# Input projection by Strassen's seven half products in two passes of 1024 tokens

## The chip, the cores and the metric

The kernel runs on one core of one Trainium2 chip. A core has TensorE (PE; its weight loads are shown as PEld), VectorE (DVE), ScalarE (ACT), GpSimd (POOL) and SyncE (SP), which here issues the DMAs. The metric is device time in microseconds (us) of one launch; lower is better.

## The reference

One inference step of a decoder layer in float32, for 2048 prompt tokens and 8 sampled tokens, model width 1024. Cut to what matters:

```python
u = _rmsnorm(h, pre_g) @ w_in                 # 1024 -> 11264 columns
aq, ak, av, az, bq, bf, bi, bz, cq, cz, ga, gb, gc = jnp.split(u, IN_OFFSETS, axis=-1)
# A: 3 groups of 8 heads of 64, (window, dilation) = (128,1), (512,4), (2048,16); rotary q, k
aq, ak = _rope(aq, pos), _rope(ak, pos)
for g in range(3):                            # 128-query blocks against (previous block, own block)
    o_g, lse_g = attend(g, aq[:, :, g], ak[:, :, g], av[:, :, g])
alpha = softmax(stack(lses)); ya = sum(alpha * outs) * silu(az)
# B: HGRN2 gated recurrence, 4 heads, state 128x128
ob, S_fin = _hgrn2(bq, (1 - lb) * sigmoid(-bf), bi, log(lb + (1 - lb) * sigmoid(bf)), S0)
yb = headnorm(ob) * silu(bz)
# C: cross-attention of 4 heads of 128 into 256 memory tokens
yc = softmax(cq @ mk.T * 128 ** -0.5) @ mv * silu(cz)
merged = sigmoid(ga) * (ya @ w_pa) + sigmoid(gb) * (yb @ w_pb) + sigmoid(gc) * (yc @ w_pc)
out = h + _rmsnorm(merged @ w_out, post_g)
```

The outputs are `out` for both kinds of tokens, the rotated keys and the values of the last rows of each window, the HGRN states and the memory's keys and values. Nearly all of the arithmetic is in the product of the first line.

## The kernel before

Every large product is made in high precision from three rounded ones: both factors are cut into a high part (rounded to F32R, the format that PE takes at full rate) and a low part (the rest), and `mm3` issues high x high, high x low and low x high for each of the eight slices of 128 input rows (lines L163 to L165). ACT makes the high part (L200 for weights) and POOL the low part (L201); for tokens these are L247 and L248.

The work goes in stages.

1. *Values* (V): eight units of 256 columns of `w_v`, token-major, tile by tile of 128 tokens. In the first two units the tokens are normalised on the way (`Prep`: squares, DVE reduction L231, a matmul with ones L233, `rsqrt` L145 to L149, eight DVE products L245, split). Memory keys and values come beside the next four units. The values of sampled tokens are small matmuls (L281).
2. *Queries and keys* (QK): 12 units of 256 columns of `w_t`, feature-major. A unit has two blocks of 128 features, each for five chunks of tokens (512, 384, 384, 384 and 392, the last with the sampled tokens), by lines L402 to L404:

```python
for k in range(KT):
    hi, lo = (t[:, k % 2, jc] for t in pieces[k // 2])
    T.matmul(ps[:, :w], lhsT=hi, rhs=xh[c][:, k, :], start=(k == 0), stop=False)
    T.matmul(ps[:, :w], lhsT=hi, rhs=xl[c][:, k, :], start=False, stop=False)
    T.matmul(ps[:, :w], lhsT=lo, rhs=xh[c][:, k, :], start=False, stop=(k == KT - 1))
    if k < KT - 1:
        yield 3 * w * PE_COL, None
```

   The rotation takes from PSUM, on DVE, a product with the cosines (L450) and a shuffle (L451), and then on POOL a product with the sines (L452) and an addition (L455).
3. *Gates* (G): 24 more units of `w_t`. Beside them, in this order, go attention (96 steps of two heads and two blocks of 128 queries), HGRN (4 heads x 4 spans of 512 tokens, 16 items), cross-attention (32 half steps), and the sampled tokens. A planner interleaves them on PE: each of these generators yields what its matmuls cost and the least time until its next turn (`ATT_GAP` and the like), and a loop issues side work as soon as it is due and projection matmuls otherwise. PE's order is the written order; the other engines' orders are made by the scheduler.
4. Branch products with the merge gates, then the output projection (again `mm3`, with L1276 and L1277 for the parts of its inputs).

An attention step loads queries and keys in float32 from DRAM and cuts them on DVE (high part of the queries L540, of the keys L544, low parts L545 and L546). Keys are stacked as [high; low] on the two halves of the partitions, so one matmul of all 128 rows makes two of the products (L575 and L576, eight a step). Then come the mask and minimum on DVE (L580), the exponential on ACT (L582), transposes on PE (L595) with a copy on ACT (L597), and products with the values, 64 columns wide (L611), copied by DVE (L614). After each pair of heads a merge (`merge`, L695 and others) weighs the three groups, with statistics `stC` and outputs `uT` that come back from DRAM.

PSUM has eight banks: three for the projection (`gps`), the others for the side work.

## Time and profile before

| | |
|---|---|
| Median of 3 runs | 3179.59 us (3176.21 to 3181.13) |
| Span of the profiled execution, from its first instruction to its last | 3169.3 us |
| Mean PE clock granted | 0.98 of full |
| Busy share of the span | PE 95%, PEld 87%, DVE 48%, ACT 31%, POOL 32% |
| DMA | 400 MB, queues busy 43% of the time of 16 engines |

No other time of the profiled execution is given; its span lies 10.3 us below the median of the runs. The busy time of PE is an end that the profile models, so the distance between the starts of matmuls is the better measure of their rate. A group line reads: line, engine, operation, tile written and tiles read, shapes, count | busy time, mean ns of one | time the engine stood idle just before them, and what ended it. A timeline row gives start and duration in us. In a row of waits the numbers are the total in us, the times, and the longest.

### The profile page before, as it was taken

The numbers are of one execution on the slowest core, as the hardware profiler recorded it, in microseconds if no ns is written. First come the engines' busy times: TensorE is split into PE (matmuls) and PEld (weight loads), VectorE is DVE, ScalarE is ACT, GpSimd is POOL, SyncE is SP. The second block draws the span as 40 slices with busy tenths as digits, with TensorE's granted clock in tenths as the row PEclk, the third lists the DMA queues.
The fourth block names the chain that finished last, engine by engine and source line by source line (L and its number), as shares of the span: only waits on it lengthen the run. The fifth ranks groups of instructions, "written<-read, shape, count | busy, mean of one in ns | idle before, by whom it ended". The sixth has DMA issues, their size and how long they took to land. (4 is left out here: it accounts for less than half of the span.)

```text
span 3169.3 us, 56318 instructions
## 1 busy us (share of the span) xinstructions
PE 3023.6 (95%) x21644; PEld 2768.5 (87%) x21644; DVE 1530.8 (48%) x3827; ACT 993.0 (31%) x2468; POOL 1021.2 (32%) x836
## 2 busy tenths in 40 slices
PE   6999999999999999999989999999998988999998
PEld 6999999999999987878878888888886778899986
DVE  8700002222224776777772277777757356233232
ACT  4412110000003654434552244444443433201222
POOL 4312126556663211111222231112125125634411
PEclk9999999999999999999989999999999999999999
DMA  4332222112123567767675323233246467665442
GB/s 137 103 97 88 72 78 75 68 67 80 67 80 111 134 168 188 170 170 191 166 170 153 108 88 97 84 99 98 89 127 180 116 164 216 199 175 176 156 146 95
DMA packets 383134, 400.11 MB, mean 126 GB/s; under 512 B 89416, under 2 KB 306120, under 8 KB 379536
## 3 DMA queue, kind: packets, MB, share of 16 engines
q1 hardware_dynamic: 382864, 396.50, 43.3%
q8 instruction: 170, 2.79, 0.4%
q14 instruction: 100, 0.82, 0.1%
HBM read 257.71 MB, written 138.67 MB: 125 GB/s over the span
## 5 line engine op out<-in xcount | busy, mean ns | idle before, releaser
L402 PE MATMUL bank<-rnd 128*128 128x384 f32 (+2 forms) x2880 | 1033.8, 359 | 13.8 <-ACT side L479 7.6
L404 PE MATMUL bank<-rnd 128*128 128x384 f32 (+2 forms) x2880 | 1010.1, 351 | 6.4 <-POOL rnd L201 6.4
L403 PE MATMUL bank<-rnd 128*128 128x384 f32 (+2 forms) x2880 | 1010.2, 351 | 0.0
L402 PEld LDWEIGHTS bank<-rnd 128*128 128x128 f32 x2880 | 550.3, 191 | 43.3 <-ACT side L479 7.9
L404 PEld LDWEIGHTS bank<-rnd 128*128 128x128 f32 x2880 | 548.3, 190 | 32.2 <-POOL rnd L201 7.6
L403 PEld LDWEIGHTS bank<-rnd 128*128 128x128 f32 x2880 | 549.6, 191 | 23.3 <-issue 1.9
L163 PE MATMUL bank<-rnd 128*128 128x256 f32 (+4 forms) x1648 | 532.4, 323 | 8.4 <-DVE raw L1249 4.2
L165 PE MATMUL bank<-rnd 128*128 128x256 f32 (+4 forms) x1648 | 529.2, 321 | 3.5 <-POOL rnd L248 3.4
L164 PE MATMUL bank<-rnd 128*128 128x256 f32 (+4 forms) x1648 | 529.5, 321 | 1.9 <-POOL rnd L1228 1.2
L201 POOL TENSOR_TENSOR rnd<-raw,rnd 128x512 fp32r<-128x512 f32 x172 | 227.7, 1331 | 557.2 <-ACT rnd L200 550.9
L163 PEld LDWEIGHTS bank<-rnd 128*128 128x128 f32 (+1 forms) x1648 | 313.4, 190 | 25.2 <-ACT rnd L1214 3.6
L165 PEld LDWEIGHTS bank<-rnd 128*128 128x128 f32 (+1 forms) x1648 | 313.4, 190 | 17.3 <-POOL rnd L248 4.6
L164 PEld LDWEIGHTS bank<-rnd 128*128 128x128 f32 (+1 forms) x1648 | 313.6, 190 | 15.4 <-POOL rnd L1228 1.5
L200 ACT CAST rnd<-raw 128x512 fp32r<-128x512 f32 x172 | 105.4, 618 | 647.5 <-PE bank L403 449.3
L450 DVE TENSOR_TENSOR raw<-bank,raw 128x384 f32<-128x384 f32 (+2 forms) x120 | 70.4, 586 | 444.1 <-POOL side L455 179.3
L582 ACT ACTIVATE raw<-raw 128x256 f32<-128x256 f32 (+1 forms) x384 | 173.2, 453 | 157.4 <-DVE raw L580 156.5
L695 POOL TENSOR_TENSOR side<-side 128x512 f32<-128x512 f32 x32 | 51.6, 1614 | 334.5 <-DMA side<-stC 271.1
L1249 DVE TENSOR_TENSOR raw<-raw,bank 128x412 f32<-128x412 f32 (+1 forms) x120 | 67.3, 580 | 169.2 <-PE bank L165 93.7
L495 ACT ACTIVATE side<-side 128x384 f32<-128x384 f32 (+2 forms) x120 | 65.4, 545 | 241.1 <-DVE side L494 235.0
L491 POOL TENSOR_TENSOR side<-side 128x384 f32<-128x384 f32 (+2 forms) x60 | 67.8, 1129 | 226.7 <-ACT side L490 205.4
L580 DVE CUSTOM_DVE_ANT_0 raw<-bank,c_amask 128x256 f32<-128x256 f32 (+1 forms) x384 | 119.6, 358 | 18.0 <-PE bank L576 8.3
L286 DVE COPY raw<-bank 8x64 f32<-8x64 f32 x32 | 7.0, 220 | 246.3 <-PE bank L281 245.5
(267 smaller groups left out, 4260.8 us busy)
## 6 DMA issues: line engine op xcount, KB each, us to landing
raw<-in_w_t SPq DMA_DIRECT2D x144, 256.0 KB
raw<-qT SPq DMA_DIRECT2D x192, 128.0 KB
raw<-sgT SPq DMA_DIRECT2D x96, 206.0 KB
sgT<-side SPq DMA_DIRECT2D x72, 192.0 KB
qT<-side SPq DMA_DIRECT2D x12, 1028.0 KB
out_kT<-side SPq DMA_DIRECT2D x12, 1028.0 KB
out_vN<-raw SPq DMA_DIRECT2D x96, 128.0 KB
raw<-out_vN SPq DMA_DIRECT2D x96, 128.0 KB
```

The source lines that it names most:

```text
L163: T.matmul(out, lhsT=lh, rhs=rh, start=(i == 0), stop=False)
L164: T.matmul(out, lhsT=lh, rhs=rl, start=False, stop=False)
L165: T.matmul(out, lhsT=ll, rhs=rh, start=False, stop=(i == n - 1))
L200: A.copy(hi, raw)
L201: G.tensor_tensor(lo, raw, hi.bitcast(F32), op=ALU.subtract)
L402: T.matmul(ps[:, :w], lhsT=hi, rhs=xh[c][:, k, :], start=(k == 0), stop=False)
L403: T.matmul(ps[:, :w], lhsT=hi, rhs=xl[c][:, k, :], start=False, stop=False)
L404: T.matmul(ps[:, :w], lhsT=lo, rhs=xh[c][:, k, :], start=False, stop=(k == KT - 1))
L450: V.tensor_tensor(t1[:, :w], ps[:, :w], rc[:, c0:c0 + w], op=ALU.mult)
L491: G.tensor_tensor(ow, ow, ew, op=ALU.mult)
L580: V.tensor_tensor_reduce(sm[:, :w], s[:, h, :w], amask[:, m0:m0 + w], -0.125, 1.0e38, ALU.add, ALU.min, accum_out=nmc)
L582: A.activation(sm[:, :w], sm[:, :w], AF.Exp, scale=-1.0, bias=nmc, accum_out=sts[hp][:, g, 1, h, idx:idx + 1])
```

## The change

The projection becomes one level of Strassen's scheme in Winograd's form. Tokens are taken in two passes of 1024, weights in 44 units of 256 columns (`w_in`; values, HGRN values, queries, keys, gates). Per unit and pass, the tokens have two halves of 512, the columns two blocks of 128, and the 1024 input rows two halves of 512. Seven products of a combination of weights (`prep_w`) with a combination of tokens (`X[0]` to `X[6]`) stand in place of eight; each is 4 slices x 3 matmuls of 512 columns (L578, L580, L581), 84 matmuls a unit. Four outputs per unit come from sums: s1 is copied out of PSUM by ACT (L586), and u2, u3, c22 and twice more u3 and u2 are added by DVE (L589 to L603), of which one output is read from PSUM and three from SBUF by what follows (`product`).

- The combinations of weights are four operations of 128x512 a unit: on DVE for the values, queries and keys, on POOL for the gates (L317 to L324). The split is done per half product, four half products ahead (`AHEAD`): ACT L219, POOL L220.
- Pass 2's combinations of tokens are made beside units 1 to 4 of pass 1 (`next_tokens`), stored in DRAM (`xc`), and loaded during the last unit of pass 1.
- Values are now feature-major and go through transposes (`turn_values`, 256 in all).
- Sampled tokens are left out of the chunks; in pass 1 each unit has 16 small matmuls on four column groups of PE, with weights as they come (`sampled`).
- Rotation: shuffle L440, both products on DVE (L442, L443), addition on POOL (L448); each finished block of 1024 is cut into parts (ACT, and DVE by L220) and stored as two parts (`qkhl`).
- Attention loads the two parts and has no cuts on DVE. Queries and keys of two heads lie on rows 0 to 63 and 64 to 127, and its scores are three products per head and block on 64 rows each, the two heads in turn (L707). A step loads its own previous block of keys and values again.
- Order: pass 1 has memory, 32 attention steps, 8 HGRN items, and half of the cross-attention with the sampled tokens; pass 2 has 64 attention steps, 8 items and the other half. The projection holds before the queries of pass 2 until pass 1's mixers are through, and pass 2's mixers begin with its gates.
- The planner's numbers: `PE_COL` 0.4219e-3 to 0.4427e-3, `ATT_GAP` 3.0 to 2.6, `SA_GAP` 2.0 to 1.8, cost of scores 0.86 to 0.72; buffers for `u` in attention 2 to 1.

The diff, cut to its core:

```diff
-            for n, (j, c) in enumerate(order):
-                ps = gps.tile([128, 512], F32, tag="g", name="ps_g")
-                for k in range(KT):
-                    ...
+    def projection():
+        gb = Banks(banks[:3], 3)
+        for n in range(2 * U_END):
+            ps_n, u = divmod(n, U_END)
+            if n == U_END:
+                yield "hgrn"
+            if u == U_Q:
+                if ps_n:
+                    yield "all"
+                rope_tables(n)
+            for o in range(7):
+                prep_w(7 * n + o + AHEAD)
+                if o == 0 and n + 1 < 2 * U_END:
+                    load_raw(n + 1)
+                wh, wl = slots.pop(7 * n + o)
+                xh, xl = X[o]
+                if o in (0, 1, 4, 5):
+                    accs[o] = gb.tile([128, HALF], F32, tag="g", name="ps_g")
+                p = accs[(0, 1, 0, 1, 4, 5, 4)[o]]
+                for k in range(4):
+                    T.matmul(p, lhsT=wh[:, k, :], rhs=xh[:, k, :], ...)
+                    T.matmul(p, lhsT=wh[:, k, :], rhs=xl[:, k, :], ...)
+                    T.matmul(p, lhsT=wl[:, k, :], rhs=xh[:, k, :], ...)
+                if o == 0:
+                    A.copy(s1, p)
+                elif o == 1:
+                    V.tensor_tensor(u2, p, s1, op=ALU.add)
+                elif o == 2:
+                    product(n, 0, 0, p, True)
+                elif o == 3:
+                    V.tensor_tensor(u3, p, s1, op=ALU.add)
+                elif o == 4:
+                    V.tensor_tensor(c22, p, u3, op=ALU.add)
+                    product(n, 1, 1, c22, False)
+                elif o == 5:
+                    V.tensor_tensor(u3, p, u3, op=ALU.add)
+                    product(n, 0, 1, u3, False)
+                else:
+                    V.tensor_tensor(u2, p, u2, op=ALU.add)
+                    product(n, 1, 0, u2, False)
...
+    def prep_w(s):
+        E = V if n % U_END < U_AZ else G
+        if o == 1:
+            E.tensor_tensor(t1, b12, b11, op=ALU.subtract)
+            E.tensor_tensor(t2, b22, t1, op=ALU.subtract)
+        elif o == 3:
+            E.tensor_tensor(b12, b22, b12, op=ALU.subtract)
+        elif o == 5:
+            E.tensor_tensor(unit_t[n][1], b21, unit_t[n][1], op=ALU.subtract)
+        split(h, l, src, G)
...
     # rotation, per output of 128x512
-                V.tensor_tensor(t1[:, :w], ps[:, :w], rc[:, c0:c0 + w], op=ALU.mult)
-                V.stream_shuffle(sh[:, :w], ps[:, :w], SHUF)
-                G.tensor_tensor(sh[:, :w], sh[:, :w], rs_[:, c0:c0 + w], op=ALU.mult)
+            V.stream_shuffle(sh, src, SHUF)
+            V.tensor_tensor(t1, src, qk["rope_c"][:, tt], op=ALU.mult)
+            V.tensor_tensor(sh, sh, qk["rope_s"][:, tt], op=ALU.mult)
...
     # attention
-            V.tensor_copy(qh, q)
-            for h in range(2):
-                V.tensor_copy(km[hi, h, sl, :], kv[hi])
-                V.tensor_tensor(km[lo, h, sl, :], kv[hi], km[hi, h, sl, :].bitcast(F32), op=ALU.subtract)
-            V.tensor_tensor(ql, q, qh.bitcast(F32), op=ALU.subtract)
...
-                    T.matmul(o, lhsT=qh[:, h, bb], rhs=km[:, h, ks, :], start=True, stop=False)
-                    T.matmul(o, lhsT=ql[:, h, bb], rhs=km[:, h, ks, :], start=False, stop=True)
+                for j, (y, z) in enumerate(((0, 0), (0, 1), (1, 0))):
+                    for h in range(2):
+                        hr = slice(64 * h, 64 * h + 64)
+                        T.matmul(ss[h][:, b, :w], lhsT=q[hr, y, bb], rhs=k[hr, z, kk], start=(j == 0), stop=(j == 2))
...
     # planner
+            if not streams and phases and (progress[0] >= U_AZ):
+                wait = len(phases) <= 3 and progress[0] < U_END + U_AZ
+            if held and (len(phases) > 3 or held == "all" and streams):
+                now = min(x[1] for x in streams)
+                continue
```

What the change moves, at three places. First DVE in a unit of queries, before:

```order
L450 TENSOR_TENSOR raw<-bank_97,raw 128x512
L451 STREAM_SHUFFLE raw<-bank_97 128x512
L450 TENSOR_TENSOR raw<-bank_98,raw 128x384
L451 STREAM_SHUFFLE extra<-bank_98 128x384
L450 TENSOR_TENSOR raw<-bank_96,raw 128x384
L451 STREAM_SHUFFLE raw<-bank_96 128x384
```

And DVE in a unit of queries now (pass 1); `bank_134` to `bank_136` are the projection's three banks, L317 to L324 combinations of weights, L594 to L603 sums of half products, L440 to L443 the rotation:

```order
L594 TENSOR_TENSOR raw<-bank_134,raw 128x512
L324 TENSOR_TENSOR raw<-raw 128x512
L597 TENSOR_TENSOR raw<-bank_135,raw 128x512
L440 STREAM_SHUFFLE raw<-raw 128x512
L442 TENSOR_TENSOR raw<-raw 128x512
L443 TENSOR_TENSOR raw<-raw 128x512
L600 TENSOR_TENSOR raw<-bank_136,raw 128x512
L322 TENSOR_TENSOR raw<-raw 128x512
L611 COPY small<-bank_141 128x256
L603 TENSOR_TENSOR raw<-bank_135,raw 128x512
L317 TENSOR_TENSOR raw<-raw 128x512
L220 TENSOR_TENSOR flex_f<-flex_f 128x1024
```

Two operations per output, both from PSUM, became sums that read PSUM with operations of two SBUF sources between them, in one queue.

Second, PE in an attention step, before; `bank_99` takes value products, `bank_103` and `bank_102` transposes, `bank_100` and `bank_101` scores, `bank_96` the projection:

```order
L611 MATMUL bank_99<-raw 64x128 x4
L595 MATMUL bank_103<-ident,raw 128x128 x2
L595 MATMUL bank_102<-ident,raw 128x128 x2
L575 MATMUL bank_100<-r_8119 128x128
L576 MATMUL bank_100<-r_8119 128x128
L575 MATMUL bank_101<-r_8119 128x128
L576 MATMUL bank_101<-r_8119 128x128
L402 MATMUL bank_96<-rnd 128x384
```

And now, with scores into `bank_137` (first head) and `bank_138` (second head):

```order
L744 MATMUL bank_141<-raw 64x128 x4
L744 MATMUL bank_141<-flex_f,raw 64x128 x4
L730 MATMUL bank_139<-ident,raw 128x128 x2
L730 MATMUL bank_140<-ident,raw 128x128 x4
L707 MATMUL bank_137<-flex_r 128x128
L707 MATMUL bank_138<-flex_r 128x128
L707 MATMUL bank_137<-flex_r 128x256
L707 MATMUL bank_138<-flex_r 128x256
L578 MATMUL bank_134<-rnd 128x512
```

The scores' rows alternate between the heads; the places of transposes and value products in a step are the same.

Third, PE at the end of the projection, before (`bank_103` takes the sampled tokens' cross-attention, L163 is the first branch product):

```order
L402 MATMUL bank_96<-rnd 128x392
L403 MATMUL bank_96<-rnd 128x392
L404 MATMUL bank_96<-rnd 128x392
L1127 MATMUL bank_103<-c_sel_c,f_15564 128x32
L163 MATMUL bank_98<-rnd 128x412
```

And now (L897, L923 and L928 are HGRN levels, L853 its norm, L953 to L982 its ends, L1017 and L1039 cross-attention):

```order
L581 MATMUL bank_136<-rnd 128x512
L953 MATMUL bank_139<-ident,flex_f 128x128 x4
L897 MATMUL bank_137<-raw 32x32 x8
L897 MATMUL bank_138<-raw 32x32 x8
L960 MATMUL bank_140<-raw 128x128 x4
L964 MATMUL bank_139<-raw,flex_f 128x128 x4
L982 MATMUL bank_140<-flex_f 128x128 x4
L853 MATMUL bank_141<-flex_f,ones_v 128x256
L923 MATMUL bank_139<-flex_f,raw 32x32 x8
L928 MATMUL bank_139<-flex_f,raw 64x64 x4
L1017 MATMUL bank_137<-ident,flex_f 128x128 x8
L1039 MATMUL bank_138<-flex_f 128x256 x2
```

The levels of two HGRN items, the ends of three and the whole second half of the cross-attention stand behind the projection's last matmul; before, all of it stood ahead of it.

More of the change, by code (lines that the diff above doesn't have):

```diff
@@ L149, in rsqrt @@
         V.tensor_tensor(out, out, tmp, op=ALU.mult)
-    sbuf = ctx.enter_context(tc.tile_pool(name="sbuf", bufs=1))
-    psum = ctx.enter_context(tc.tile_pool(name="psum", bufs=1, space=PSUM))
-    rnd = sbuf.tile([128, int(152.5 * 256)], F32R, name="rnd")
-    raw_ = sbuf.tile([128, int(26.5 * 256)], F32, name="raw")
-    banks = [psum.tile([128, 512], F32, name=f"bank{i}") for i in range(8)]
-    def pool(name):
-        return tc.tile_pool(name=name, bufs=1, reuse_waits="tile")
-    def mm3(out, pairs):
-        n = len(pairs)
-        for i, (lh, ll, rh, rl) in enumerate(pairs):
-            T.matmul(out, lhsT=lh, rhs=rh, start=(i == 0), stop=False)
-            T.matmul(out, lhsT=lh, rhs=rl, start=False, stop=False)
-            T.matmul(out, lhsT=ll, rhs=rh, start=False, stop=(i == n - 1))
@@ L501, in until @@
-    def until(u):
-        while progress[0] < u:
-            yield 0.0, 1.0
-    def attention(ap, pool, rnd8, spawn):
-        steps = [(hp, g, sg) for hp in range(4) for g in range(3) for sg in range(8)]
-        sts = {}
-        loaded = {}
+    xs = const.tile([128, KT, 32], F32, name="xs")
+    small = const.tile([128, 448], F32, name="small")
+    sts = [const.tile([128, 3, 2, 2, 16], F32, name=f"a_st{h}") for h in range(4)]
+    X0, W0, RND = 0, 112, 132
+    RAW0, T0, C0, S0, ALL = 0, 12, 16, 30, 43
@@ new lines, in tile_hybrid_step, with flexed, mm3 @@
+    ctx.callback(lambda: flex["pool"].close())
+    def flexed(rounded):
+        return [(flex["r"], 0, flex["at"])] if rounded else [(flex["f"], 0, FLEX - flex["at"])]
+    lay_out(0)
+    banks = [psum.tile([128, 512], F32, name=f"bank{i}") for i in range(8)]
+    def mm3(out, pairs):
+        n = len(pairs)
+        for i, (lh, ll, rh, rl) in enumerate(pairs):
+            T.matmul(out, lhsT=lh, rhs=rh, start=(i == 0), stop=False)
+            T.matmul(out, lhsT=lh, rhs=rl, start=False, stop=False)
+            T.matmul(out, lhsT=ll, rhs=rh, start=False, stop=(i == n - 1))
@@ L1154, in tile_hybrid_step, with sample @@
-    extra = []
+    first = [(hp, g, sg) for hp in range(4) for g in range(2) for sg in (range(4) if g == 0 else range(0, 8, 2))]
+    second = [(hp, g, sg) for hp in range(4) for g in range(3)
+              for sg in (range(4, 8) if g == 0 else range(1, 8, 2) if g == 1 else range(8))]
+    po_bank = banks[7][:, 0:256]
+    sel = {}
+    def sample(sps, sp):
+        yield from until(U_G + 2)
+        for key in ("sel_a", "sel_c"):
+            sel[key] = sp.tile(list(I[key].shape), F32, name=key, bufs=1)
+            dma(sel[key], I[key])
+        yield from sample_heads(sps, sp)
+        yield from sample_attention(sps, sp)
+        yield from sample_hgrn(sps, sp)
+        yield from sample_cross(sps, sp)
@@ new lines, in memory_phase, with attention_phase, phase, hgrn_phase @@
+    def memory_phase(spawn):
+        lay_out(FLEX)
+        spawn(memory(Banks(banks[3:4]), Banks(banks[4:6])))
+    def attention_phase(part):
+        def phase(spawn):
+            lay_out(12)
+            spawn(attention(Banks(banks[3:7]), po_bank, side(), Region(*flexed(True)), second if part else first, spawn))
+        return phase
+    def hgrn_phase(part):
+        def phase(spawn):
+            lay_out(0)
+            spawn(hgrn(Banks(banks[3:7]), side(), part, spawn))
+        return phase
@@ L1157, in tile_hybrid_step, with cross_phase, phase @@
+    def cross_phase(part):
+        def phase(spawn):
+            spawn(cross(Banks(banks[3:7]), Region((flex["f"], 0, 22.125), bufs=2), part))
+            if part == 0:
+                spawn(sample(Banks([banks[7][:, 0:256]]), Region((raw_, S0, ALL), (flex["f"], 22.125, FLEX), bufs=1)))
+        return phase
+    phases = [memory_phase]
+    for part_ in range(2):
+        phases += [attention_phase(part_), hgrn_phase(part_), cross_phase(part_)]
     if True:
-        main = gate_stream(Region((side, 0, 6), bufs=2))
+        main = projection()
```

953 lines of the change are left out of this document (515 added, 438 removed).

## The prediction

> **What bounds the kernel now.** I read the page's busy shares first, then a table of windows cut at the first and last matmul of each phase, then the same windows for one projection line, then the timeline for spacings.
>
> ```profile
> PE 3023.6 (95%) x21644; PEld 2768.5 (87%) x21644; DVE 1530.8 (48%) x3827; ACT 993.0 (31%) x2468; POOL 1021.2 (32%) x836
> 0.00:447.50 447.50, 420.17 (x3814) 411.89 (x3815) 135.99 (x307) 127.03 (x267) 110.56 (x78) 0.98 0.32 96
> 447.50:997.00 549.50, 549.50 (x2965) 525.58 (x2965) 142.02 (x372) 33.34 (x54) 325.10 (x317) 1.00 0.22 77
> 997.00:1683.00 686.00, 644.96 (x4439) 564.06 (x4438) 488.81 (x1578) 351.96 (x1135) 128.47 (x97) 0.97 0.65 166
> 1683.00:1813.00 130.00, 118.81 (x631) 112.97 (x630) 31.59 (x46) 26.02 (x50) 34.33 (x24) 0.97 0.46 130
> 1813.00:2331.00 518.00, 513.09 (x5941) 455.42 (x5939) 376.48 (x790) 220.69 (x441) 106.53 (x79) 1.00 0.30 93
> 2331.00:2693.00 362.00, 318.80 (x1609) 280.94 (x1607) 211.34 (x447) 144.91 (x347) 130.13 (x110) 0.95 0.59 167
> 2693.00:2975.00 282.00, 273.05 (x1440) 269.32 (x1441) 87.91 (x136) 45.30 (x59) 151.11 (x116) 0.99 0.63 187
> 2975.00:3170.00 195.00, 185.25 (x818) 148.35 (x816) 56.67 (x152) 43.74 (x117) 35.02 (x18) 0.98 0.36 115
> ```
>
> The columns are window, length, busy time of PE, PEld, DVE, ACT and POOL, granted clock, DMA share, GB/s. The rows are: values (V); queries and keys (QK); projection with attention; with merges; with HGRN; with cross-attention and the sampled tokens; branch products; output. PE is full everywhere at a clock of 0.95 to 1.00, so this kernel is a sum of matmuls plus small gaps, and no other engine passes 73% in a stage. How much of each stage is projection, the same windows say for L402 alone, one of three equal lines:
>
> ```profile
> 447.50:997.00 549.50, 342.60 (x987) 185.25 (x987) 1.00 0.22 77
> 997.00:1683.00 686.00, 225.01 (x622) 122.35 (x623) 0.97 0.65 166
> 1813.00:2331.00 518.00, 245.99 (x669) 125.27 (x668) 1.00 0.30 93
> 2331.00:2693.00 362.00, 146.57 (x394) 77.49 (x393) 0.95 0.59 167
> ```
>
> In QK nothing else runs: 549.5/987 = 0.557 us per triple of matmuls. Subtracting count x 0.557 leaves what a stage pays beside the projection: attention (686 - 346)/96 steps = 3.54 us a step; HGRN (518 - 373)/16 items = 9.1; cross and sampled tokens 143, or 4.46 for each of 32 half steps; merges about 13 in all. From the timeline of PE:
>
> ```profile
> 249.79 0.28 PE L164 MATMUL bank<-rnd 128*128 128x256 f32 x1
> ...
> 254.23 0.28 PE L165 MATMUL bank<-rnd 128*128 128x256 f32 x1
> ...
> 803.53 0.40 PE L402 MATMUL bank<-rnd 128*128 128x512 f32 x1
> ...
> 808.99 0.33 PE L402 MATMUL bank<-rnd 128*128 128x384 f32 x1
> ...
> 814.21 0.33 PE L402 MATMUL bank<-rnd 128*128 128x384 f32 x1
> ```
>
> Between the two first rows lie 37 starts, between the next 24 and 30: 0.120 us a matmul of 256, 0.2275 of 512, 0.174 of 384. Time goes with columns.
>
> **The projection.** Removed: 3072 matmuls of 256 (368.6) and 36 units of 80 triples at 0.557 (1604): 1973. Added: 88 units of 84 matmuls of 512 at 0.2275 = 19.11 each, 1682. The gain from seven products for eight is 291 us, before anything gets in its way. I add 0.5 to a unit (19.6) for the 16 small matmuls of the sampled tokens and for starts. What could get in its way is the preparation, on DVE and POOL (first DVE's busy tenths in 40 slices of 79 us, then groups of lines with their mean in ns, then the timeline):
>
> ```profile
> DVE  8700002222224776777772277777757356233232
> L201 POOL TENSOR_TENSOR rnd<-raw,rnd 128x512 fp32r<-128x512 f32 x172 | 227.7, 1331 | 557.2 <-ACT rnd L200 550.9 <-DMA f<-szT 2.6 <-PE bank L576 1.6
> L455 POOL TENSOR_TENSOR side<-raw 128x512 f32<-128x512 f32 x12 | 15.6, 1304 | 0.9
> L1277 DVE TENSOR_TENSOR rnd<-side,rnd 128x1024 fp32r<-128x1024 f32 x8 | 9.8, 1225 | 51.1 <-ACT rnd L1276 51.1
> L546 DVE TENSOR_TENSOR r<-raw,r 128x512 fp32r<-128x512 f32 x96 | 70.1, 730 | 2.0
> L545 DVE TENSOR_TENSOR r<-raw,r 64x256 fp32r<-64x256 f32 x192 | 91.5, 476 | 5.9
> L544 DVE CAST r<-raw 64x256 fp32r<-64x256 f32 x192 | 66.3, 345 | 44.8 <-DMA raw<-out_kT 25.3 <-PE bank L576 14.7 <-DMA side<-uT 1.7
> L540 DVE CAST r<-raw 128x512 fp32r<-128x512 f32 x96 | 42.6, 444 | 5.5 <-POOL side L458 5.5
> 61.57 2.41 POOL L248 TENSOR_TENSOR rnd<-raw,rnd 128x1024 fp32r<-128x1024 f32 x1 [4.12 <-ACT rnd L247]
> 62.48 1.64 DVE L146 TENSOR_TENSOR raw<-raw 128x128 f32<-128x128 f32 x1
> 64.16 0.29 DVE L147 TENSOR_TENSOR raw<-raw 128x128 f32<-128x128 f32 x1
> ```
>
> The last three rows are the price of the conflict. A 128x128 product with two SBUF sources takes 0.29 us alone (L147); the one started beside POOL (L146) took 1.64 and ended at 64.12, 0.14 after POOL's 63.98. It waited POOL out. [...]
>
> A QK unit (two features blocks, four outputs of 512) now has on POOL seven splits at 1.331 and four rope additions at 1.304 = 14.5, and on DVE eleven two-source operations of 512 at 0.73 (four weight combinations, seven rope products) and two splits of 1024 at 1.225 = 10.5. (POOL's 14.5 stands against 325.1/12 = 27 for a unit twice the size today.) Full addition gives 25.0 a unit; full overlap leaves PE's 19.6. Some POOL work overlaps DVE's shuffles and reads of PSUM, so I take 24 operations x 0.15 less, 21.4, and 22.1 with the short deadlines named below: 24 units, 530. Units outside QK have 9.3 us of splits on POOL and up to 2.9 on DVE, which fit under 19.6.
>
> - First unit: before, DVE was busy eight and seven tenths in the first two slices, 158 us, while 16 token tiles were normalised, about 9.9 a tile (an estimate: 158/16). The seven sides need all eight tiles before the second half product: 8 x 9.9 + 6 x 2.7 = 95.
> - Values, seven more units of pass 1: 256 transposes in all, at 0.11 by the weight loads in the spacing below, 1.8 a unit; preparing pass 2's tokens beside units 1 to 4 is bounded by 0 and 79 (eight pairs of tiles, if PE waited all of the 9.9 on each); I take 22, nearer the lower end, since PE has other units' work: 7 x 21.4 + 22 = 172.
> - The other 56 units: 56 x 19.6 + 14 of transposes = 1112.
> - Memory keys: 192 matmuls x 0.12 + 10 = 33. Reload of the sides and the hold before pass 2's rope: 14.
>
> **Attention.** The four kinds of splits leave DVE: (91.5 + 66.3 + 42.6 + 70.1)/96 = 2.82 us a step, at a DVE share of 71%. PE keeps transposes, 6.25 a step, and value products, 12.5. The first row is what PE waits for today:
>
> ```profile
> 1239.67 0.33 PE L575 MATMUL bank<-r 128*128 128x128 f32 x1 [0.74 <-DVE r L545]
> 1244.34 1.12 PE L611 MATMUL bank<-raw 128*64 128x128 f32 x16
> 138.72 0.63 PE L281 MATMUL bank<-raw 128*8 128x64 f32 x32
> L595 PE MATMUL bank<-ident,raw 128*128 128x128 f32 x600 | 101.8, 291 | 20.8 <-ACT raw L582 17.9
> 1237.67 0.86 PEld L595 LDWEIGHTS bank<-ident,raw 128*128 128x128 f32 x8 [0.17 <-issue]
> ```
>
> Transposes 101.8/600 = 0.17 (loads alone 0.86/8 = 0.11), value products 1.12/16 = 0.07. With scores as six pairs at 0.12 each: 0.72 + 1.06 + 0.87 = 2.65 a step, 254. No row has row halves. For them speaks L281: column tiles of 64 columns start (0.63 - 0.22)/31 = 0.013 us apart, under half of 64 columns' 0.03. Against: L611, 64-column halves at 0.057, no faster than whole-width columns, as each loads fresh weights. Bounds 2.65 and the present 3.54; I take the lower, as the loads come from separate partitions. [...]
>
> Loads grow from 0.62 to 0.98 MB a step by the shapes, at a DMA share of 0.65 in this stage; SP's queue issues them in one row with each unit's four weight loads; a late one is in the waits below. The stored parts of queries and keys double that stage's writes, and pass 2's sides are written beside the values: DMA shares of 0.22 and 0.32 there cover both, so nothing. Gone with that cover they would delay only the first loads of attention, units later.
>
> **The rest.** HGRN beside units: 14 x 9.1 + 15 for DVE's combinations = 142. First half of cross 16 x 4.46 = 71, sampled tokens 18. After the last projection matmul nothing covers the last two items, at DVE's 376.5/16 = 23.5 each, some 10 of finishing, and 16 half steps of cross, 71: 128. Branch and output stay, 477 + 8 for weights prepared beside the tail's DMA. Short deadlines: a bank of PSUM is written again one half product (2.73) after DVE or ACT must have read it; with heavier loads I put 40 on all such waits (0 to 100).
>
> Sum: 95 + 172 + 530 + 1112 + 33 + 14 + 254 + 142 + 89 + 128 + 485 + 40 = 3094. That is a span; the profiled one is 3169.3, 10.3 under the median 3179.6, so 3104.
>
> **Rivals.**
> [...]
> - Slower: the conflict adds up in full and behind it POOL's splits miss PE: QK 25.0 a unit (+70), HGRN +30, values +25: 3229. It decides where a QK unit passes about 25 us. The L146 row speaks for it; that POOL's operations before were mostly lone speaks against.
> - POOL held by the merges' loads, so that weight splits queued behind come late:
>
> ```profile
> POOL side L695 <- DMA side<-stC: 271.1, 22, 44.7
> ```
>
>  It waited 12.3 on average; weights are ready four half products ahead, 11 us. Some ten waits of 8 us: 3184.
> - The change does not do what it says in the scores: halves run one after another, twelve at 0.12 and not six: +0.72 x 96 = 69, 3173. [...]
>
> **How the numbers follow.** Main case 0.50, its own range 3035 to 3165 (waits 0 to 100, attention to 3.54, tokens' preparation 0 to 79). Hidden conflict 0.14; full conflict 0.16; POOL held 0.10; serial halves 0.10. The forecast is the main case, 3104. The range is 2975 to 3235: below it lies about 0.10 (most of the hidden conflict), above it 0.09 (the full conflict with its waits on top). Measured differences under 0.2% (6 us) say nothing. Faster: 0.14 + 0.47 of the main case + half of serial halves = 0.66; same 0.02 + 0.03 + 0.03 = 0.08; slower 0.16 + 0.07 + 0.03 = 0.26.
>
> **What would show it.** Projection matmuls 0.2275 apart and 7392 of them; QK at 22 us a unit, POOL near 65%, with DVE operations that end right after POOL's; first unit over at 95; attention at 2.65 us a step beside the units, with paired starts on the score line; about 128 us between the last projection matmul and the first branch product. I am wrong if QK is at 25 or PE waits on weight splits elsewhere too, or if score halves start 0.1 apart one by one.

## The result, and the profile after

The changed kernel takes 3620.87 us (median of 4 runs, 3619.15 to 3622.32) against 3180.36 for the kernel before beside it: a ratio of 1.1386, 95% interval 1.1365 to 1.1408. It is slower by 14%, where 3104 had been forecast. The profiled execution spans 3617.3 us at a mean granted clock of 0.918 (0.982 before). Beside this run and those below, the kernel before took 3170 to 3180 us (medians), so differences of less than 10 us between two runs say nothing. Two executions, one of e6 (4142 us at a granted clock of 0.65) and one of e10 (12731 us at 0.20), are left out of the times below.

The busy shares first, then windows over the phases, cut at the first matmul of a phase's first unit; the columns are those of the prediction's table.

```profile
PE 3051.9 (84%) x19206; PEld 2413.7 (67%) x19206; DVE 2108.1 (58%) x4095; ACT 1318.7 (36%) x2966; POOL 1749.5 (48%) x1307
0.00:110.90 110.90, 54.02 (x304) 44.91 (x305) 78.41 (x171) 42.03 (x86) 42.28 (x36) 0.74 0.31 83
110.90:319.60 208.70, 177.23 (x973) 135.92 (x972) 124.89 (x219) 78.96 (x148) 93.40 (x67) 0.93 0.56 162
319.60:626.50 306.90, 267.62 (x1448) 207.22 (x1447) 262.74 (x380) 77.02 (x119) 180.59 (x132) 0.97 0.38 122
626.50:795.80 169.30, 137.42 (x813) 111.77 (x813) 67.00 (x106) 59.29 (x113) 113.76 (x85) 0.91 0.43 131
795.80:995.00 199.20, 199.20 (x1622) 152.62 (x1621) 84.36 (x332) 128.03 (x386) 78.35 (x62) 1.00 0.62 185
995.00:1354.70 359.70, 304.18 (x3172) 232.83 (x3171) 280.09 (x492) 158.31 (x317) 181.97 (x140) 0.93 0.29 87
1354.70:1776.30 421.60, 341.51 (x1524) 265.18 (x1523) 244.89 (x440) 136.10 (x288) 220.41 (x177) 0.88 0.57 175
1776.30:2057.20 280.90, 248.97 (x1017) 200.21 (x1016) 233.89 (x309) 78.56 (x120) 178.57 (x131) 0.94 0.43 138
2057.20:2571.70 514.50, 430.97 (x2756) 317.69 (x2755) 216.31 (x739) 239.30 (x769) 204.58 (x153) 0.88 0.75 203
2571.70:2755.70 184.00, 153.61 (x598) 120.30 (x598) 89.10 (x112) 84.82 (x148) 137.33 (x100) 0.91 0.52 149
2755.70:2990.10 234.40, 198.80 (x2046) 155.22 (x2045) 195.11 (x316) 111.70 (x201) 124.73 (x90) 0.91 0.36 111
2990.10:3128.50 138.40, 71.22 (x697) 49.98 (x696) 87.57 (x200) 49.34 (x126) 24.17 (x18) 0.82 0.41 120
```

PE's busy time has hardly changed (3024 before), with 2438 fewer matmuls, but the time in which it is not busy went from 146 us (3169.3 - 3023.6) to 565. That PE's busy time did not fall lies in part in the clock: by the clock records of the two traces PE worked 419 us at half the rate, and 98 before, which cost it half of that, 210 and 49 us (an estimate). Only one phase, pass 1's attention, has no idle time and a clock of 1.00. DVE's busy time rose by 577 us.

The same stages against the terms of the sum, with the four experiments that price a cause (e1 without POOL's splits of weights, e10 with them on DVE, e5 without the merges' weighing, e7 without splits, pass 2's preparation and weighing). Lengths in us, each to the next stage's first matmul:

| stage (units) | forecast | after | e1 | e10 | e5 | e7 |
|---|---|---|---|---|---|---|
| first unit | 95 | 111 | 104 | 106 | 111 | 103 |
| values, pass 1 (7) | 172 | 209 | 195 | 203 | 210 | 163 |
| queries and keys, both passes (24) | 530 | 588 | 487 | 562 | 587 | 487 |
| memory (5) | 131 | 169 | 161 | 163 | 169 | 160 |
| attention, pass 1 (5, 32 steps) | 183 | 199 | 199 | 199 | 199 | 199 |
| HGRN, pass 1 (10) | 276 | 360 | 320 | 337 | 359 | 319 |
| cross, sampled tokens, values of pass 2 (12) | 352 | 422 | 385 | 401 | 419 | 388 |
| attention, pass 2 (10, 64 steps) | 366 | 515 | 498 | 497 | 416 | 410 |
| merges (7) | 137 | 184 | 171 | 173 | 145 | 141 |
| HGRN, pass 2 (7) | 199 | 234 | 210 | 220 | 232 | 212 |
| after the last unit, to the branch products | 128 | 139 | 141 | 142 | 142 | 143 |
| branch and output | 485 | 489 | 488 | 488 | 489 | 489 |
| waits, not placed | 40 | | | | | |

The forecast column is the prediction's terms, with 19.6 for each unit that stands in a stage.

**Where PE waits.** A unit of queries in pass 1, timeline rows of DVE, POOL and PE; then the clock after the wait:

```profile
445.21 1.28 POOL L220 TENSOR_TENSOR rnd<-raw,rnd 128x512 fp32r<-128x512 f32 x1 [1.33 <-ACT rnd L219]
445.31 1.73 DVE L442 TENSOR_TENSOR raw<-raw 128x512 f32<-128x512 f32 x1
446.96 0.68 DVE L443 TENSOR_TENSOR raw<-raw 128x512 f32<-128x512 f32 x1
447.56 0.68 DVE L603 TENSOR_TENSOR raw<-bank,raw 128x512 f32<-128x512 f32 x1
448.38 0.47 PE L578 MATMUL bank<-rnd 128*128 128x512 f32 x1 [2.21 <-DVE raw L603]
...
448.92 0.39 PE L581 MATMUL bank<-rnd 128*128 128x512 f32 x1
449.15 0.55 PE L578 MATMUL bank<-rnd 128*128 128x512 f32 x1
...
450.35 0.63 PE L578 MATMUL bank<-rnd 128*128 128x512 f32 x1
450.77 0.63 PE L580 MATMUL bank<-rnd 128*128 128x512 f32 x1
...
452.79 0.39 PE L578 MATMUL bank<-rnd 128*128 128x512 f32 x1
448.40:452.70 4.30, 4.30 (x12) 3.40 (x13) 3.15 (x3) 2.05 (x3) 3.23 (x3) 0.60 0.30 85
```

A product that takes 0.68 us (L443) starts 0.1 after a POOL split and takes 1.73 (L442). The trace has 328 such operations of 128x512, both sources in SBUF, among the rotation's products and the combinations of weights. The 125 of them that began while POOL worked took 1.74 us (median), and 105 of these ended 0.5 to 0.6 us after POOL's operation; the others took 0.68. The sums L589 to L603, which read one source from PSUM, took 0.68 beside POOL and alone (144 and 296 of them), and the rotation's shuffles (L440) 0.75 and 0.73. So it is the product that waits, and not DVE as a whole. The sum behind it (L603), which must read its bank before PE may write there, is late, and PE stands 2.21 us. Then 12 matmuls take 4.3 us and not 2.7, at a granted clock of 0.60 (0.23 apart at first, 0.42 at 450.35): the wait is paid again in clock. The low parts of the weights themselves were hardly ever late: PE waited for POOL's splits 1.6 us in all.

```profile
PE bank L580 <- POOL rnd L220: 1.6, 2, 0.9
```

**What went as planned.** The row halves run side by side. One step's scores now and before, from the first score to the next projection matmul:

```profile
899.34 0.98 PE L707 MATMUL bank<-flex_r 64*128 64x256 f32 x12
900.25 0.50 PE L578 MATMUL bank<-rnd 128*128 128x512 f32 x1
...
1247.77 0.36 PE L575 MATMUL bank<-r 128*128 128x256 f32 x1
...
1248.80 0.34 PE L402 MATMUL bank<-rnd 128*128 128x384 f32 x1
```

Twelve half matmuls in 0.91 us against eight whole ones in 1.03: 0.12 us a step, and not the 0.24 of six against eight, since the group of halves loses about 0.1 at both of its ends.

### The profile page after: what moved, and what is told of

It is laid out like the page before. It is cut to its first block, busy times and chain, and to the rows that moved or that the text cites. A ratio compares the mean times of both kernels' runs of the same rounds, so it can differ in the third digit from the quotient of the medians.

```text
span 3617.3 us, 54250 instructions
## 1 busy us (share of the span) xinstructions
PE 3051.9 (84%) x19206; PEld 2413.7 (67%) x19206; DVE 2108.1 (58%) x4095; ACT 1318.7 (36%) x2966; POOL 1749.5 (48%) x1307
## 5 line engine op out<-in xcount | busy, mean ns | idle before, releaser
L220 POOL TENSOR_TENSOR rnd<-raw,rnd 128x512 fp32r<-128x512 f32 x621 | 834.2, 1347 | 922.9 <-ACT rnd L219 844.3
L578 PE MATMUL bank<-rnd 128*128 128x512 f32 x2464 | 1073.1, 436 | 190.3 <-DVE raw L589 60.3
L580 PE MATMUL bank<-rnd 128*128 128x512 f32 x2464 | 1013.9, 411 | 1.6 <-POOL rnd L220 1.6
L581 PE MATMUL bank<-rnd 128*128 128x512 f32 x2464 | 1009.6, 410 | 0.0
L578 PEld LDWEIGHTS bank<-rnd 128*128 128x128 f32 x2464 | 494.6, 201 | 340.9 <-issue 95.7
L219 ACT CAST rnd<-raw 128x512 fp32r<-128x512 f32 x626 | 379.6, 615 | 644.5 <-PE bank L580 444.8
L581 PEld LDWEIGHTS bank<-rnd 128*128 128x128 f32 x2464 | 493.4, 200 | 115.0
L580 PEld LDWEIGHTS bank<-rnd 128*128 128x128 f32 x2464 | 495.6, 201 | 92.6 <-POOL rnd L220 2.6
L213 PE MATMUL bank<-rnd 128*128 128x412 f32 (+3 forms) x692 | 256.6, 371 | 1.8 <-ACT rnd L1441 0.9
L717 ACT ACTIVATE raw<-raw,a_st 128x256 f32<-128x256 f32 (+1 forms) x384 | 172.7, 451 | 227.5 <-DVE a_st L715 227.5
L215 PE MATMUL bank<-rnd 128*128 128x412 f32 (+3 forms) x692 | 255.0, 368 | 0.0
L214 PE MATMUL bank<-rnd 128*128 128x412 f32 (+3 forms) x636 | 237.0, 373 | 11.2 <-POOL rnd L1442 10.0
L448 POOL TENSOR_TENSOR flex_f<-raw 128x512 f32<-128x512 f32 x96 | 132.3, 1378 | 140.6 <-DVE raw L443 126.8
L715 DVE CUSTOM_DVE_ANT_0 raw<-bank,c_amask 128x256 f32<-128x256 f32 (+1 forms) x384 | 117.4, 361 | 96.9 <-PE bank L707 88.6
L1428 POOL TENSOR_TENSOR raw<-raw 128x412 f32<-128x412 f32 (+1 forms) x80 | 89.1, 1114 | 129.5 <-DVE raw L1424 128.9
L730 PE MATMUL bank<-ident,raw 128*128 128x128 f32 x600 | 111.3, 303 | 42.2 <-ACT raw L717 38.3
L213 PEld LDWEIGHTS bank<-rnd 128*128 128x128 f32 (+1 forms) x692 | 129.4, 187 | 18.5 <-ACT rnd L1441 3.8
L219 ACT CAST flex_f<-flex_f 128x1024 fp32r<-128x1024 f32 (+1 forms) x64 | 60.3, 942 | 218.1 <-POOL flex_f L448 196.5
L215 PEld LDWEIGHTS bank<-rnd 128*128 128x128 f32 (+1 forms) x692 | 129.7, 187 | 13.3
L214 PEld LDWEIGHTS bank<-rnd 128*128 128x128 f32 (+1 forms) x636 | 119.1, 187 | 27.9 <-POOL rnd L1442 12.8
```

The costliest lines, as they stand in the source:

```text
L213: T.matmul(out, lhsT=lh, rhs=rh, start=(i == 0), stop=False)
L214: T.matmul(out, lhsT=lh, rhs=rl, start=False, stop=False)
L215: T.matmul(out, lhsT=ll, rhs=rh, start=False, stop=(i == n - 1))
L219: A.copy(h, src)
L220: eng.tensor_tensor(l, src, h.bitcast(F32), op=ALU.subtract)
L448: G.tensor_tensor(st.rearrange("p (r l) -> p l r", r=d)[:, half * m:half * m + m, :], t1.rearrange("p (l r) -> p l r", r=d), sh.rearrange( ...
```

## The experiments

**e1: what POOL's splits cost.** Leaves POOL's splits of weights out; `wlow` is one constant tile.

```diff
-        l = wring.tile([128, 4, 128], F32R, tag="wl", name="wl")
-        split(h, l, src, G)
+        l = wlow
+        A.copy(h, src)
```

> Leaves out POOL's 616 splits of weights in the changed kernel: the high part is still cut by ACT, and every product with a low part of the weights uses one constant tile. PE has the same matmuls. Theory A (DVE's operations with two SBUF sources wait out POOL's splits, and PE waits on the sums behind them): DVE's rotation products fall from 1.0 to 0.7 us, a unit of queries from 26.2 (pass 1) and 23.9 (pass 2) to about 20, the two stages of queries and keys from 588 to about 490, DVE's busy time by 200 us or more, and the whole to 3300 to 3400. [...]

3369.46 us, ratio to before 1.0622 (1.0603 to 1.0641), 251 us less than the changed kernel. Theory A, in its range, and in its place: units of queries fell to 21.2 in pass 1 and 19.3 in pass 2. DVE's groups in units of queries of pass 1, after and then e1 (L444 and L445 of e1 are L442 and L443; L323 and L318 are the combinations L322 and L317), then two rows of PE in e1's pass 1 (the sampled tokens' matmuls), and the windows of e1's two stages of queries and keys:

```profile
L443 DVE TENSOR_TENSOR raw<-raw 128x512 f32<-128x512 f32 x36 | 34.6, 962 | 0.0
L442 DVE TENSOR_TENSOR raw<-raw 128x512 f32<-128x512 f32 x27 | 28.3, 1046 | 0.3
L322 DVE TENSOR_TENSOR raw<-raw 128x512 f32<-128x512 f32 x9 | 12.9, 1431 | 0.0
L317 DVE TENSOR_TENSOR raw<-raw 128x512 f32<-128x512 f32 x9 | 6.2, 692 | 10.1 <-POOL rnd L220 10.1
...
L445 DVE TENSOR_TENSOR raw<-raw 128x512 f32<-128x512 f32 x40 | 28.4, 711 | 0.0
L444 DVE TENSOR_TENSOR raw<-raw 128x512 f32<-128x512 f32 x30 | 22.5, 750 | 0.4
L323 DVE TENSOR_TENSOR raw<-raw 128x512 f32<-128x512 f32 x9 | 6.1, 680 | 0.0
L318 DVE TENSOR_TENSOR raw<-raw 128x512 f32<-128x512 f32 x9 | 11.2, 1245 | 0.0
...
L339 PE MATMUL bank<-raw,xs 128*32 128x128 f32 x384 | 15.5, 279 | 0.0
L521 PE MATMUL bank<-c_sel,small 128*128 128x8 f32 x48 | 6.1, 235 | 0.0
298.80:554.20 255.40, 255.40 (x1449) 202.28 (x1448) 212.40 (x385) 79.94 (x120) 69.34 (x50) 1.00 0.46 146
1618.40:1850.50 232.10, 232.03 (x1016) 188.86 (x1014) 209.69 (x313) 78.82 (x120) 68.32 (x49) 1.00 0.53 166
```

In the two windows PE has no idle time at a clock of 1.00, though DVE is still 83 to 90% busy. DVE's busy time over the whole kernel fell by 244 us (2108.1 to 1864.0) with the same 4095 operations. One combination got slower, 1245 ns (L318) where it had taken 692 (L317). POOL's rotation addition, which e1 keeps, is the likely cause: in the changed kernel 28 of the 125 operations began beside it (L448) and took 1.74 us too. Only 100 of the 251 us lie in queries and keys; 64 lie in HGRN, the rest in most of the other stages.

The two windows also price something else. The units of pass 1 take 21.2 us and those of pass 2 19.3, and neither waits for anything: the 1.9 us between them are the sampled tokens' small matmuls (L339 and L521, which only pass 1 has) and the slower starts around them. In the changed kernel (L338 and L519) a group of 16 of their trace rows, two a unit, lengthens the projection's run of starts by 0.79 us, and one of four by 0.47.

**e2: later deadlines.** The half products in another order, and seven banks for queries and keys.

```diff
+ORDER = (0, 1, 4, 2, 3, 5, 6)
...
-            for o in range(7):
+            for i, o in enumerate(ORDER):
...
-                    accs[o] = gb.tile([128, HALF], F32, tag="g", name="ps_g")
+                    accs[o] = (gb7 if U_Q < u < U_AZ else gb3).tile([128, HALF], F32, tag="g", name="ps_g")
```

> The seven half products in the order 0, 1, 4, 2, 3, 5, 6, so that the first sums have two half products (5.5 us) before their bank is written again and not one, and seven PSUM banks in place of three in the units of queries and keys. The work is the same. Theory A (DVE has no time to spare in these units, so that a later deadline only moves the wait): units of queries stay within 1 us of 26.2 and 23.9, the whole at 3570 to 3625. Rival B (each sum is late for its own deadline only, and short waits then cost a slower clock): units of queries fall to about 21 to 22, and the whole by 100 or more, to 3470 to 3520.

3607.17 us, ratio 1.1374 (1.1352 to 1.1395), against 1.1386: the same time, as theory A says. Units of queries take 25.4 us in pass 1 and 23.1 in pass 2 on average, against 25.6 and 23.4. The waits changed their line and little else.

**e3: one buffer in the merges.**

```diff
-                w = pool.tile([128, 512], F32, tag="mw", name="a_mw", bufs=1)
+                w = pool.tile([128, 512], F32, tag="mw", name="a_mw", bufs=2)
```

> The merges' weights get two buffers, as in the kernel before, and not one. Theory A (with one buffer each load starts after the last use, DVE's queue stands at the merge for the transfer, and the masks of the scores stand behind it): pass 2's attention falls from 514 to about 430, the idle time ahead of the merge's addition on DVE (L830, 114 us in that stage) to a third, the whole by 80 to 110, to 3510 to 3540. Rival B (the transfers are late because the DMA engines are at 0.75 there): the stage stays at 490 to 514 and the whole at 3590 or more.

3584.4 us, ratio 1.1293 (1.1268 to 1.1318), 36 less; pass 2's attention 515 to 494. Between the two: neither theory's number. (The list of the change above doesn't name that these weights went from two buffers to one.) The single buffer is a part of it, but the merges' transfers stay late with two. How they reach PE, from the changed kernel (timeline rows of DVE, POOL and PE in one step):

```profile
2414.65 0.44 PE L744 MATMUL bank<-raw 128*64 128x128 f32 x4
2416.69 1.52 POOL L829 TENSOR_TENSOR flex_f<-flex_f 128x512 f32<-128x512 f32 x1 [4.65 <-DMA flex_f<-stC]
2418.24 1.04 DVE L830 TENSOR_TENSOR flex_f<-flex_f 128x512 f32<-128x512 f32 x1 [5.32 <-POOL flex_f L829]
2419.19 0.28 DVE L715 CUSTOM_DVE_ANT_0 raw<-bank,c_amask 128x128 f32<-128x128 f32 x1
2420.07 1.63 PE L730 MATMUL bank<-ident,raw 128*128 128x128 f32 x4 [4.76 <-ACT raw L717]
```

POOL waits for the load of the weights (`stC`), DVE's addition for POOL, and the masks of the scores (L715), which need nothing of the merge, stand behind that addition in DVE's queue; then exponential, then PE's transposes, 4.76 us late.

**e4: pass 2's tokens.** Leaves out `next_tokens` and `next_pass`; pass 2 multiplies pass 1's tokens.

```diff
                     if n == U_END - 1:
-                        next_pass(o)
+                        pass
...
-                    if 1 <= n <= 4:
-                        next_tokens(n, o)
```

> Leaves out the preparation of pass 2's tokens beside units 1 to 4 and the reload of the sides: pass 2 multiplies pass 1's tokens again. Expected of every theory: units 2 to 4 of pass 1 fall from 37 to 24 us, and the last unit and the first units of pass 2 by some us, 45 to 60 in all, 3560 to 3575. If the reload of 14.7 MB also delayed pass 2's first units (45, 29, 37 and 60 us now), 80 or more.

3569.55 us, ratio 1.125 (1.1232 to 1.1268): 51 less, 46 of it in units 1 to 7. As expected.

**e5: the merges' weighing.** Each merge keeps its turns and one load and store.

```diff
             for g in range(3):
-                dma(u, uT[g, hp] ...)
-                dma(w[64 * h:64 * h + 64], stC[hp, g, h:h + 1, tc_] ...)
-                V.tensor_tensor(acc, acc, w, op=ALU.mult)
-                G.tensor_tensor(uv, uv, nat(w, d), op=ALU.mult)
-                V.tensor_tensor(nat(acc, d), nat(acc, d), uv, op=ALU.add)
                 yield 0.0, M_GAP
             dma(z, szT[hp, :, tc_])
-            V.tensor_tensor(acc, acc, z, op=ALU.mult)
-            dma(yT[hp, :, tc_], acc)
+            dma(yT[hp, :, tc_], z)
```

> Leaves out the weighing in the merges of the changed kernel: each merge keeps its turns and its last load and store, but not the loads of outputs and weights nor the DVE and POOL work on them. Theory A (it is the merges, by their waits in DVE's queue and by their transfers together, that make pass 2's attention cost 4.98 us a step beside the units where pass 1's costs 3.2): the stage falls from 514 to about 400 to 420, the merges' stage from 184 to about 150, the whole by 120 to 150, to 3470 to 3500. Rival B (pass 2's attention is slow by its own loads beside the gates' stores): the stage stays above 470 and the whole above 3550.

3474.51 us, ratio 1.0957 (1.0936 to 1.0977), 146 less. Theory A, and nearly all of it in two stages: attention of pass 2 to 416, merges to 145.

```profile
DVE side L696 <- POOL side L695: 36.6, 15, 4.8
...
DVE flex_f L830 <- POOL flex_f L829: 113.9, 22, 9.0
...
2054.00:2470.00 416.00, 383.49 (x2756) 294.44 (x2754) 167.19 (x700) 243.25 (x775) 168.20 (x131) 0.95 0.75 217
```

The first row is DVE's wait at the merges' addition beside attention in the kernel before (96 steps), the second the same in the changed kernel (64 steps), the third e5's window of that attention: the DMA share is as high as before, 0.75, yet PE is idle for 33 us and not 84. So the load on the DMA engines is not the cause by itself; what is queued behind the late transfers is the likelier one. e5 also takes away the merges' own work on DVE and POOL (DVE's busy time in this stage falls from 216 to 167 us), and no run parts that work from the wait.

**e6, e8, e9: the attention part alone**, in the kernel before: parts cut once in the stage of queries and keys, pairs of 64 rows. The diff is e6's, cut to its core; its scores are those of the change's diff. e6 has the change's single buffer for a step's output, e8 two (UB = 2), e9 also the old gap (ATT_GAP = 3.0).

```diff
+                        A.copy(h, st[:, cp])
+                        V.tensor_tensor(l, st[:, cp], h.bitcast(F32), op=ALU.subtract)
+                        dma(qkhl[j, 0, :, cp], h.bitcast(F32))
+                        dma(qkhl[j, 1, :, cp], l.bitcast(F32))
...
-            split(i)
+            q, k = loaded.pop(i)
...
-UB = 2
+UB = 1
-ATT_GAP = 3.0
+ATT_GAP = 2.6
```

> The kernel before, with the attention part of the change alone: the parts of rotated queries and keys are cut once in the stage of queries and keys (ACT and DVE, 96 pieces of 512) and stored, attention loads them and makes its scores as pairs of 64 rows, with ATT_GAP 2.6 and a cost of scores of 0.72. Nothing of the projection changes. Theory A (the pairs run side by side at 0.82 us a step and DVE's four splits are gone): attention falls from 3.54 us a step to about 3.0 to 3.1, the stage from 686 to 635 to 645, the stage of queries and keys stays within 10 of 549, the whole at 3125 to 3145, faster than before. Rival B (the larger loads at a DMA share above 0.65 make the steps wait): the stage stays at 680 or more and the whole at 3175 to 3220.

> The attention part alone in the kernel before, as e6, with two buffers for a step's output (u) and not one. In e6 DVE stood 79 us at the copy of the output for the store of the step before, and masks stood behind it. Theory A (that one buffer is what the attention part loses): PE's waits on the exponential (25 us) go, the whole falls from 3210 to 3170 to 3190. Rival B (larger loads are what it loses; DVE would wait anyway): 3200 to 3215.

> As e8, with ATT_GAP back at 3.0: the planner leaves 15% more between steps, so more projection lies beside attention. Theory A (a step's chain through DVE and ACT is longer than the planner leaves at 2.6): another 10 to 25 us off, 3150 to 3175, at or below the kernel before. Rival B (the chain fits; what is left are transfers): within 5 us of e8.

e6 3209.64 us, ratio 1.0114 (1.0093 to 1.0135); e8 3215.61, 1.0131 (1.0108 to 1.0154); e9 3191.23, 1.0062 (1.0043 to 1.0081). Every form is slower than before, by 0.6 to 1.3%. e6 and e8 lie in the ranges of their rivals B: the second buffer does nothing. The wider gap of e9 brings back some 20 us, as its theory A says, but not the level that it forecast. The stage of queries and keys, and attention from its first score to its last product with values, before and e9; the two rows of attention hold the same 621 triples of projection matmuls:

```profile
447.30:981.30 534.00, 534.00 (x2883) 511.04 (x2882) 135.03 (x357) 30.19 (x49) 317.85 (x310) 1.00 0.21 74
996.90:1682.20 685.30, 644.26 (x4433) 563.53 (x4433) 488.33 (x1576) 351.68 (x1135) 128.23 (x97) 0.97 0.65 167
...
447.20:992.50 545.30, 536.93 (x2883) 510.01 (x2882) 209.36 (x449) 86.23 (x141) 317.38 (x309) 1.00 0.38 137
1023.90:1697.70 673.80, 640.31 (x4816) 542.32 (x4818) 240.26 (x1009) 347.61 (x1126) 120.82 (x94) 0.97 0.70 199
PE bank L571 <- DMA r<-qkhl: 17.9, 3, 15.7
```

DVE's busy time in attention halves, 488 to 240, and attention gets 11.5 us shorter, 0.12 a step. That is what the shorter scores alone would give (0.12 x 96), and also what PE had waited for the splits before (11.6 us: L576 8.2, L575 3.4); which of the two it was, no run shows. So nearly all of the work that DVE was spared had not been on PE's path. What is new is more: 11 us in the stage of queries and keys and one wait of 15.7 for the first loaded parts.

**e7: three causes at once.** The edits of e1, e4 and e5 together.

> Leaves out three things of the changed kernel at once: POOL's splits of weights (one constant low part), the preparation of pass 2's tokens, and the weighing in the merges. If their costs add (251 and 51 measured, about 130 for the merges): 3621 - 432 = 3190, still above the 3104 of the forecast, the rest being HGRN, cross-attention and sampled tokens that wait on DVE. If they share waits: 3230 to 3280. If one wait hides behind another: under 3150.

3212.94 us, ratio 1.0124 (1.0102 to 1.0145): 408 less, against 448 for the sum of the three: between two of the forecasts, some waits are shared.

**e10: the splits on DVE.** All the work is kept; 616 splits go from POOL to DVE.

```diff
-        split(h, l, src, G)
+        split(h, l, src, V)
```

> The changed kernel with its 616 splits of weights on DVE and not on POOL. The splits then cost DVE 0.73 us each, 450 in all, where e1 priced them on POOL at 251 in all, 0.41 each. Theory A (DVE waits out every POOL operation that overlaps one of its own, so moving it saves that wait and pays 0.73): units of queries of pass 2 go from 23.9 to about 22.8 (17.7 + 7 x 0.73), but HGRN, where DVE is at 82 to 98%, gets longer; the whole between 3560 and 3700. [...]

3490.24 us, ratio 1.1004 (1.0967 to 1.1042): 131 less, below the range of theory A and 121 above e1. Units of queries of pass 2 fell to 22.5, near A's 22.8; HGRN got shorter (360 to 337 in pass 1) where A had it longer. The first rows of the pages of e1, e10 and e12, and DVE's group of splits in e10:

```profile
PE 2967.4 (88%) x19206; PEld 2363.7 (70%) x19206; DVE 1864.0 (56%) x4095; ACT 1321.8 (39%) x2967; POOL 925.7 (28%) x691
PE 3016.8 (86%) x19206; PEld 2392.3 (69%) x19206; DVE 2268.2 (65%) x4711; ACT 1322.1 (38%) x2966; POOL 953.4 (27%) x691
PE 3020.5 (96%) x21644; PEld 2768.2 (88%) x21644; DVE 1560.1 (49%) x3923; ACT 995.9 (32%) x2468; POOL 892.1 (28%) x740
L220 DVE TENSOR_TENSOR rnd<-raw,rnd 128x512 fp32r<-128x512 f32 x621 | 519.8, 839 | 141.7 <-ACT rnd L219 131.1 <-PE bank L494 6.6 <-issue 2.1
```

DVE took 616 more operations, which took 0.84 us each and not 0.73, some 517 in all, and its busy time rose by 160: its other operations got some 357 us shorter (in the queries of pass 2 L442 went from 1137 to 718 ns, L443 from 954 to 682). What had counted there as busy was waiting for POOL; that is A's mechanism. e1 and e10 both also empty POOL's queue, in which the rotation's additions stand, and no run parts what that is worth from the waits of DVE.

**e11: three mends together**, the edits of e10, e3 and e2.

> The changed kernel with three things mended together, all of the work kept: splits of weights on DVE (e10, -128 alone), two buffers for the merges' weights (e3, -36 alone), the half products in the order of e2 with seven banks for queries and keys (-13 alone). If they add: 3621 - 177 = 3444. If e2's later deadlines are worth more once DVE no longer waits for POOL (units of queries of pass 2 at 22.5 and not 23): 3400 to 3430. In either case it stays above the kernel before, since the merges' weighing (146 in all) and HGRN's load on DVE remain.

3476.99 us, ratio 1.0972 (1.0945 to 1.0999): 13 less than e10, where the two other mends had saved 36 and 14 alone, and in neither forecast's range. Once DVE waits less for POOL, they have little left to save.

**e12: the mend in the kernel before.** The splits of its last 24 units on DVE.

```diff
-                G.tensor_tensor(lo, raw, hi.bitcast(F32), op=ALU.subtract)
+                (V if self.dve else G).tensor_tensor(lo, raw, hi.bitcast(F32), op=ALU.subtract)
```

> The kernel before, with the splits of weights of the 24 gate units (96 operations of 128x512) on DVE and not on POOL, the one mend of the changed kernel that carries over. Theory A (the conflict with POOL's splits costs DVE 0.4 us each and PE waits for part of it): 96 x 0.4 = 39 us of DVE's waits go against 70 us of added work; in the attention stage, at a DVE share of 71%, nothing is gained, and the whole stays within 6 us of 3175. Rival B (in HGRN and attention DVE's lateness is mostly that conflict): 3145 to 3165. Rival C (DVE becomes too full beside attention): 3185 to 3210.

3156.13 us against 3169.71 beside it, ratio 0.995 (0.9934 to 0.9966): faster than both kernels, though by 0.5% only, in the range of theory B. DVE's busy time went from 1530.8 to 1560.1, 29 for 69 of added work (96 splits at 0.72): some 40 us of waits went, as A's arithmetic said, but PE did profit, most of it in attention, whose last value product starts 10 us earlier (1672.1 against 1682.2).

## Why the prediction was wrong, point by point

The kernel takes 517 us more than the 3104 of the forecast. Without POOL's splits, the merges' weighing and pass 2's tokens (e7) it is 408 us shorter; of these three the sum had a part of the first, nothing for the second and 36 for the third.

- *The half products: right; the small matmuls beside them: too low.* There are 7392 matmuls at 0.2275, and where nothing disturbs them a unit of pass 2 takes 19.3 to 19.6 (e1; the unit at 1776 us in the changed kernel). The 291 us are there. But to each unit 0.5 was added for the sampled tokens' matmuls and for starts, and e1 shows 1.9 more in a unit of pass 1 than in one of pass 2: 21.2 where 19.6 was counted, some 70 us in 44 units, of which pass 2's lower 19.3 gives back some 13.
- *The conflict of DVE with POOL: the step that failed, in its size.* It was priced in 24 units of queries alone (+2.5 a unit), with the words that units outside have 9.3 us of POOL's splits and 2.9 of DVE's, "which fit under 19.6". e1 measured 251 us over all stages. The mistake was to compare sums of busy time with a unit's length: what a split does to a DVE operation (0.68 to 1.73 us) is passed on by DVE's queue to a sum, and by the sum to PE, which may not write the bank before; a later deadline alone (e2) helped nothing. Even in the units of queries 22.1 was too low (26.2 and 23.9); the slower rival's 25.0 was nearer, though 1.9 of the 26.2 are the sampled tokens and its total, 3229, was far too low too. No run shows the terms behind the 22.1: that all of POOL's 14.5 us add to DVE's 10.5 was the author's estimate, and so was the 0.15 taken off for each of 24 operations. What the trace shows is 1.74 us (median) for 0.68 in 125 of 328 operations with two SBUF sources, and no such loss in sums and shuffles; e1 and e10 agree, and e1's 244 us of DVE's busy time are the conflict's size in this kernel, as far as POOL's splits go.
- *Waits, 40 (0 to 100): too low several times over.* Idle time grew by 419 us, and most waits of more than 1.5 us are followed by a slow clock (counted in the last section).
- *Merges: the second step that failed, left at nothing, worth 146 (e5).* The rival "POOL held by the merges' loads" had the source right and the victim wrong: not weight splits behind POOL but masks behind DVE. The kernel before has the same chain, with two buffers and a wait of 37 us where there are now 114.
- *Attention: a gain of 0.9 us a step was counted.* In pass 1, without merges beside it, PE never waits, and with 21.2 for a unit a step takes (199.2 - 106)/32 = 2.91, near the 2.65; so there the sum of the matmuls was nearly right. Pass 2 has 4.98 with 19.6 a unit, and 3.3 to 3.4 without the weighing (e5, e7). The 2.82 us of DVE splits cost PE little before, and e9 shows that the part alone makes the kernel no faster. The rival of serial halves fell: pairs run side by side (starts 3 to 4 ns apart).
- *Pass 2's tokens, 22 in a bound of 0 to 79, and 14 for the reload and the hold:* 51 for tokens and reload (e4). The first unit took 111 and not 95.
- *The end, branch and output: right* within 11 and 4 us.
- *HGRN, cross-attention, memory:* 84 + 35, 70 and 38 us over their terms. e1 took 64, 37 and 9 of these away. What is left, some 110 us in e7 over the forecast, lies in these stages and in attention. Some 38 us of it (24 units of pass 1 in memory, attention, HGRN and cross-attention at 1.6) are the sampled tokens' matmuls. For the rest, DVE at 78% over pass 1's HGRN and the sums in its queue are the likely cause; no run here isolates it, and it stays open.

## What to carry to other kernels

When a change thins the slack between engines (here sums that PE waits for in the same queue as side work), an estimate by busy sums can fail, as this one did: look in the profile for the operation whose duration has two values, and ask whose queue stands behind it. Work put on POOL to relieve DVE may cost more than leaving it on DVE: here 616 splits on POOL cost the kernel 251 us by e1, and 131 came back when DVE took them. Saving an engine's time pays only where PE waits for it: halving DVE's work in attention bought at most 12 us, and moving 96 splits to DVE, which added to its work, bought 14.
